# Layer B of a two-layer encoder: queries, keys and gates worked on in the projection's PSUM bank instead of in an SBUF copy

## The chip, the cores and the metric

The kernel runs on one core of one Trainium2 chip. The metric is the device time of one execution in microseconds (us). A core has five engines that run side by side, each through its own queue in order: PE (TensorE, matmuls and transposes), DVE (VectorE), ACT (ScalarE), POOL (GpSimd) and SP (SyncE, which here issues the DMAs). They wait for one another by semaphores. Matmul results land in PSUM, which PE, ACT and DVE reach and POOL does not.

## The reference

One inference step of a two-layer streaming encoder, model width 1024, on 2048 prompt frames and 64 sample frames. Layer A is gated sliding-window attention (16 query heads, 2 key heads, own chunk of 64 frames and 2 previous ones); layer B is gated chunk-band attention (16 heads of 64, own chunk and 8 previous ones, a learned bias by clipped distance). Both layers do

```
h = rms_norm(x, g);  q, k, v, gate = split(h @ w_in)
q = rms_norm(q, q_g) per head;  k = rms_norm(k, k_g) per head
o = softmax(q k^T / 8 + bias) v          (band of chunks; layer A with sinks)
y = x + (o * silu(gate)) @ w_out
```

and the newest keys and values are returned as caches. What matters here is layer B's path from the projection `h @ w_in` of 128 frames to normed queries and keys, and to silu(gate) = gate/2 * (tanh(gate/2) + 1).

## The kernel before, in words

Layer B works on 8 head pairs, one after the other. For each head pair it projects 16 prompt tiles of 128 frames (two tiles are a unit) and one sample tile of 64 frames, which comes between prompt tiles 13 and 14. A projection (`project`) is 24 matmuls of 128x512 for a prompt tile (lines 713 to 715, three products of high and low fp16 parts) and 16 for a sample tile (708, 709). Its 512 result columns are 128 of queries, 128 of keys, 128 of values and 128 of gate, for two heads. They fill one PSUM bank called `pj`, of which there are two: the projection after the next one writes the same bank again.

The result is evacuated by `evacuate_b`, for each of the 128 prompt tiles of the 8 head pairs: ACT copies queries and keys times a scale C_B into the SBUF tile `pa` (line 749, 256 columns, for the last four tiles of a head pair 384 with the values), then the high part of the values into `values` (753), then the gate times C_B into `pb` (761). DVE takes the low part of the values from PSUM (756). Behind that stands the norm, `head_norm` with `apart=True`, in three steps: POOL squares `pa` into `sq` (795); DVE sums the squares by head (809) and POOL adds a constant and raises to the power -1/2 (812, 813); DVE multiplies `pa` by the result in place (818). And the gate, in two steps: ACT takes tanh of half of `pb` into `sq` (832); DVE forms (tanh + 1) * gate in `pb` (838).

The order of the work is written out by hand on PE, where attention of one head pair and the projections of the next (the `filler`) are interleaved to marks. The other engines get their work in the order in which the code emits it. The small steps above are deferred: `bg.put` queues a step, and `bg.share`, called twice for each of the four score blocks of a unit, counts a turn up and runs due steps up to a budget of cost. A step put with `after=` comes at least one turn behind the one that it names, and `wait=2` means two turns. `bg.run` forces a step at once. The queries and keys are transposed by PE (904 called from `queries`, line 1422 on) once all steps of their unit are emitted.

Further lines that the text below uses: 1498 and 1499 are the score matmuls into the double PSUM buffer `sb`; 1502 is DVE's bias and minimum over a block of scores and 1507 its correction; 1514 is ACT's exponential; 1554 and 1555 split the weights of attention into high (ACT) and low (POOL); 500 and 503 split weights of the next projection (ACT, DVE); 1877 is a DVE operation of the output projection that reads PSUM; 1301 is the copy of the transposed gate; 222 a small matmul that spreads scales over the partitions. Layer A uses `head_norm` and `gate` too, and so does the sample tile.

Of the kernel before, what the change touches and what calls it, by code (L numbers as in the profile page):

```python
# [13 lines left out]
AF = mybir.ActivationFunctionType  # L14
ALU = mybir.AluOpType
AX = mybir.AxisListType

P = 128
# [7 lines left out]
NT = SEQ // P  # L26
NO = 8
OT = TOK // NO
HD = 64
# [20 lines left out]
HB, WB_, PB, VB = 2.0 ** 10, 2.0 ** 14, 2.0 ** 14, 16.0  # L50
LAG = 4
SQB = 4
# [4 lines left out]
def hybrid_encoder_kernel(  # L57
# [97 lines left out]

    most = const([P, 84], "most")
    top = const([P, 12], "top")
    scl = const([P, 9, 3], "scl")
    gsb = const([P, 8, KC], "gsb")
    S_W, C_B, G_B = (lambda h, i=i: scl[:, h, i : i + 1] for i in range(3))  # L160
# [26 lines left out]
    def times(dst, a, c):  # L187
        nc.vector.tensor_scalar(dst, a, c, 1.0, op0=ALU.mult, op1=ALU.mult)
# [30 lines left out]

    def everywhere(h, o):  # L220
        ps = tp_bank()
        nc.tensor.matmul(ps[:, 0:3], ones[0:1, 0:1].to_broadcast([1, P]), o, start=True, stop=True)

        def fn():
            nc.vector.tensor_copy(scl[:, h], ps[:, 0:3])
# [9 lines left out]

    def input_across(h):
        across(h, h + 1)
        e, r, o = row[:, 16:17], row[:, 17:18], row[:, 20:23]
        powers(row[:, h : h + 1], e, r)
        times(o[:, 0:1], r, WB_)  # L240
        times(o[:, 1:2], e, 1 / (HB * WB_))
        times(o[:, 2:3], e, 0.5 / VB if h > 0 and len(TURNED) == 2 else 0.5 / (VB * PB))

    def input_scales(h):
        everywhere(h, row[:, 20:23])

    def output_top():
        largest(8, 64, 80)
# [451 lines left out]

    def project(tile_, xc, w, C, res, ps=None):
        tt, t0, n = tile_
        ps = ps or psum("pj", 512, 2)
        for k in range(KC):
            wh, wl = weights_of(w, k)
            xh, xl = xc.parts[k // 2]
            if xl is None:
                nc.tensor.matmul(ps[:, :C], xh[:, k % 2, :], wh, start=k == 0, stop=False)
                nc.tensor.matmul(ps[:, :C], xh[:, k % 2, :], wl, start=False, stop=k == KC - 1)
                cost = 2 * C / 2400  # L710
            else:
                xh, xl = (a[:, k % 2, t0 : t0 + n] for a in (xh, xl))
                nc.tensor.matmul(ps[:n, :C], xh, wh, start=k == 0, stop=False)  # L713
                nc.tensor.matmul(ps[:n, :C], xh, wl, start=False, stop=False)  # L714
                nc.tensor.matmul(ps[:n, :C], xl, wh, start=False, stop=k == KC - 1)  # L715
# [29 lines left out]

    def evacuate_b(hp, tt, ps, g):
        a = t("pa", [P, 384], 4)
        true = a if tt >= NT - 4 else a[:, 0:256]
        nc.scalar.activation(true, ps[:, : true.shape[1]], AF.Identity, scale=C_B(hp))  # L749
        c = VB / (HB * WB_)  # L750
        v = ps[:, 256:384].rearrange("p (h d) -> p h d", d=HD)
        vh = held["VH"][:, tt]
        nc.scalar.activation(vh[:, :, 0:HD], v, AF.Identity, scale=c)

        def low():
            nc.vector.scalar_tensor_tensor(
                vh[:, :, HD:P], v, c, vh[:, :, 0:HD], op0=ALU.mult, op1=ALU.subtract
            )

        held["rest"].append(bg.put(0.2, low, True, wait=2))  # L760
        held["evac"] = nc.scalar.activation(g, ps[:, 384:512], AF.Identity, scale=C_B(hp)).ins
        return a

    def evacuate_sample(hp, ps, g):
        a = t("pa", [P, 384], 4)
# [565 lines left out]
    def layer_b():  # L1331
# [4 lines left out]
        def add_unit(hp, unit):  # L1336
# [23 lines left out]
            def gen():  # L1360
# [9 lines left out]
                for e, (tt, t0, n) in enumerate(tiles):  # L1370
# [3 lines left out]
                    if last:  # L1374
# [8 lines left out]
                        it.ready = True  # L1383
                        yield c
                        continue
                    pr = evacuate_b(hp, tt, out[0], it.gate[:, e])
                    it.prs.append(pr)
                    v, kn = pr[:n, 256:384], pr[:n, 128:256]
                    norm = head_norm(n, pr[:n, 0:256], apart=True)
                    it.todo += norm + gate(n, it.gate[:n, e], True)  # L1390
                    if it is its[0] and e == 0:
                        block_scales(TOK - OT)
                    if tt >= NT - 4:
                        o = (tt - (NT - 4)) * P
                        it.todo.append(
                            store_kv(1, slice(0, P), kn, v, kb_p[o : o + P, cols], vb_p[o : o + P, cols], norm[-1])
                        )
                    it.ready = e == len(tiles) - 1
                    scale_work(hp, u, e)
# [628 lines left out]
```

## Time and profile before

| what | value |
|---|---|
| time, median of 3 runs | 2118.7 us (2116.3 to 2124.02) |
| the profiled execution's own time | 2123.14 us |
| its span, first to last instruction | 2121.3 us |
| PE busy | 2046.8 us, 96% of the span |
| DVE, ACT, POOL busy | 1498.7, 1440.8, 1143.7 us |
| mean granted TensorE clock | 0.991 |

Layer B's attention, with the projections of its later head pairs beside it, takes about the stretch from 865 us to 1919 us of the span; the first 135 us of it belong to the first head pair, in which the activations are scaled and split as well. Busy times count one engine's instructions; matmuls are pipelined, so that PE can be busy without being at its peak. A line such as `PE tp L904 <- DVE pa L818: 4.5, 6, 2.4` in the view of waits means that PE's instructions of line 904 that write `tp` sat idle 4.5 us in total, 6 times, at most 2.4 us, until DVE's instruction of line 818 on `pa` ended.

### The profile page before, as it was taken

How to read it: one execution, taken by the hardware profiler on the slowest of the kernel's cores; microseconds unless marked ns; L12 is line 12 of the kernel's file. 1: busy time of each engine (PE TensorE's matmuls, PEld its weight loads, DVE VectorE, ACT ScalarE, POOL GpSimd, SP SyncE). 2: the span in 40 equal slices, each digit the busy share in tenths (PEclk: the TensorE clock that was granted, in tenths of full speed). 3: DMA queues.
4: the chain of work that ended last, by engine and by line, in shares of the span. 5: the costliest groups of instructions: out<-in, count | busy, mean ns of one | idle time of the engine just before them, and what ended most of it. 6: DMA issues, size and time to landing. Idle time of an engine off the chain costs nothing.

```text
span 2121.3 us, 40864 instructions
## 1 busy us (share of the span) xinstructions
PE 2046.8 (96%) x12951; PEld 1470.7 (69%) x12951; DVE 1498.7 (71%) x4049; ACT 1440.8 (68%) x3640; POOL 1143.7 (54%) x1621
## 2 busy tenths in 40 slices
PE   8999999999999999998999999999999999999999
PEld 6788788878888999655655555555555555557788
DVE  7778778768667554687768777787877778678542
ACT  6878878767777332466677677786867777677330
POOL 5655544433445445775367576676766767575000
PEclk9999999999999999999999999999999999999999
DMA  8856545766544666744469789897897969678763
GB/s 276 274 172 213 173 157 189 215 174 212 165 149 132 212 205 200 247 148 155 138 166 225 175 191 232 169 239 180 199 216 169 254 159 212 152 152 197 215 200 115
DMA packets 509593, 404.21 MB, mean 191 GB/s; under 512 B 302064, under 2 KB 446848, under 8 KB 509344
## 3 DMA queue, kind: packets, MB, share of 16 engines
q1 hardware_dynamic: 509376, 401.60, 70.1%
q8 instruction: 102, 1.67, 0.3%
q14 instruction: 115, 0.94, 0.1%
HBM read 257.59 MB, written 73.43 MB: 156 GB/s over the span
## 4 chain that ended last, share of the span: by engine, by line
PE 59%; DVE 12%; ACT 10%; DMA 6%; issue 6%; POOL 5%; SPq 0%; ACTq 0%; POOLq 0%; DVEq 0%
PE pj L713 10%; PE pj L715 10%; PE pj L714 10%; PE pj L1871 5%; PE pj L1873 5%; PE pj L1872 5%; PE o L1660 2%; PE sa L904 2%; PE tp L904 2%; DVE p L1502 2%; ACT values L1554 2%; PE sb L1498 2%; ACT p L1514 1%; PE sb L1499 1%; PE o L1256 1%
## 5 line engine op out<-in xcount | busy, mean ns | idle before, releaser
L713 PE MATMUL pj<-wh,xx 128*128 128x512 f16 (+2 forms) x1648 | 641.9, 389 | 6.0 <-ACT pb L736 2.3
L715 PE MATMUL pj<-wh,xx 128*128 128x512 f16 (+2 forms) x1648 | 624.3, 379 | 1.3 <-POOL xx L598 1.3
L714 PE MATMUL pj<-wh,xx 128*128 128x512 f16 x1024 | 389.4, 380 | 0.8 <-DVE wh L503 0.8
L1555 POOL TENSOR_TENSOR values<-p,values 128x640 f16<-128x640 f32 (+2 forms) x224 | 281.5, 1259 | 177.5 <-ACT values L1554 172.9
L1514 ACT ACTIVATE p<-p,nm 128x640 f32<-128x640 f32 (+5 forms) x264 | 199.3, 755 | 199.5 <-DVE nm L1507 150.3
L1871 PE MATMUL pj<-xx,wh 128*128 128x264 f32 (+1 forms) x1024 | 291.4, 285 | 8.4 <-DVE res L1877 3.9
L1872 PE MATMUL pj<-xx,wh 128*128 128x264 f32 (+1 forms) x1024 | 288.9, 282 | 0.0
L1502 DVE CUSTOM_DVE_ANT_0 p<-sb,BT 128x640 f32<-128x640 f32 (+5 forms) x272 | 196.6, 723 | 94.8 <-PE sb L1499 91.1
L714 PE MATMUL pj<-wl,xx 128*128 128x512 f32 (+1 forms) x624 | 234.6, 376 | 3.0 <-DVE wl L503 3.0
L598 POOL TENSOR_TENSOR xx<-xraw,xx 128x528 fp32r<-128x528 f32 (+4 forms) x144 | 185.4, 1305 | 90.8 <-ACT xx L597 84.1
L813 POOL TENSOR_TENSOR f<-f,mhalf 128x4 f32<-128x4 f32 (+2 forms) x187 | 190.4, 1019 | 11.8
L715 PEld LDWEIGHTS <-xx 128*128 128x128 f16 x1024 | 100.5, 98 | 124.5 <-issue 2.8
L1316 POOL TENSOR_TENSOR o<-gt,o 128x256 f32<-128x256 f32 (+1 forms) x132 | 103.6, 784 | 152.2 <-ACT p L1219 92.5
L818 DVE TENSOR_TENSOR pa<-pa,f 128x256 f32<-128x256 f32 (+3 forms) x221 | 145.6, 661 | 54.4 <-POOL f L813 49.9
L795 POOL TENSOR_TENSOR sq<-pa 128x256 f32<-128x256 f32 (+2 forms) x187 | 115.0, 615 | 115.1 <-ACT pa L749 80.1
L1219 ACT ACTIVATE p<-p,nm 128x257 f32<-128x257 f32 (+2 forms) x272 | 134.4, 497 | 47.4 <-DVE nm L1213 40.0
L714 PEld LDWEIGHTS <-xx 128*128 128x128 f16 x1024 | 100.5, 98 | 82.5 <-issue 4.7
L713 PEld LDWEIGHTS <-xx 128*128 128x128 f16 x1024 | 100.6, 98 | 80.7 <-ACT xx L597 1.5
L1554 ACT CAST values<-p 128x640 f16<-128x640 f32 (+2 forms) x224 | 147.3, 658 | 5.0
L1873 PE MATMUL pj<-xx,wl 128*128 128x264 f32 x512 | 145.8, 285 | 0.5 <-DVE wl L496 0.5
L1873 PE MATMUL pj<-xx,wh 128*128 128x264 f16 x512 | 142.7, 279 | 1.0 <-DVE wh L493 1.0
L1213 DVE CUSTOM_DVE_ANT_0 p<-sa,BT,nsink 128x256 f32<-128x256 f32 (+2 forms) x272 | 117.5, 468 | 35.7 <-PE sa L904 29.8
(282 smaller groups left out, 5028.9 us busy)
## 6 DMA issues: line engine op xcount, KB each, us to landing
xx<-xsb SPq DMA_DIRECT2D x112, 512.0 KB, 4.3
xx<-xsa SPq DMA_DIRECT2D x88, 512.0 KB, 4.7
xraw<-oga SPq DMA_DIRECT2D x64, 264.0 KB, 3.8
xraw<-ogb SPq DMA_DIRECT2D x64, 264.0 KB, 3.9
xsa<-xx SPq DMA_DIRECT2D x32, 512.0 KB, 4.3
wl<-in_w_in_b_dram SPq DMA_DIRECT2D x64, 256.0 KB, 5.0
wraw<-in_w_in_b_dram SPq DMA_DIRECT2D x56, 256.0 KB, 3.6
xraw<-in_x_dram SPq DMA_DIRECT2D x40, 256.0 KB, 4.2
```

The lines of the kernel that those rows point to most:

```text
L598: nc.gpsimd.tensor_tensor(lo, rv, wide(hi), op=ALU.subtract)
L713: nc.tensor.matmul(ps[:n, :C], xh, wh, start=k == 0, stop=False)
L714: nc.tensor.matmul(ps[:n, :C], xh, wl, start=False, stop=False)
L715: nc.tensor.matmul(ps[:n, :C], xl, wh, start=False, stop=k == KC - 1)
L813: nc.gpsimd.tensor_tensor(fv, fv, mhalf[:n, :H], op=ALU.pow)
L1502: mi = nc.vector.tensor_tensor_reduce(out=p[r, :nk], in0=S[r, o : o + nk], in1=b, op0=ALU.add, op1=ALU.min, scale=1.0, scalar=3e38, accum_ ...
L1514: ex = nc.scalar.activation(p[:n, :nk], p[:n, :nk], AF.Exp, scale=-1.0, bias=it.nm[:n, c : c + 1], accum_out=it.sm[:n, c : c + 1],)
L1554: hi = nc.scalar.copy(two[:, :, 0, :], pv)
L1555: lo = nc.gpsimd.tensor_tensor(two[:, :, 1, :], pv, two[:, :, 0, :], op=ALU.subtract)
L1871: nc.tensor.matmul(ps[:, :OT], wh, oh, start=k == 0, stop=False)
L1872: nc.tensor.matmul(ps[:, :OT], wh, ol, start=False, stop=False)
L1873: nc.tensor.matmul(ps[:, :OT], wl, oh, start=False, stop=k == KC - 1)
```

## The change

For 15 of the 16 prompt tiles of a head pair:

- ACT squares queries and keys straight from PSUM (`Square` of C_B times the column, 256 columns, into `sq`). The copy of queries and keys into `pa` goes, and POOL's squares with it. For the last four tiles of a head pair ACT still copies the values (128 columns).
- DVE's scaling, which multiplied `pa` in place, reads queries and keys from PSUM, multiplies by C_B and by the norm's factor, and writes `pa`.
- The gate's copy goes. ACT takes tanh from PSUM with a scale C_T (half of C_B), right in the evacuation; DVE forms (tanh + 1) * gate with the unscaled gate from PSUM. The missing factor C_B goes into G_B, the scale that the transposed gate is copied with.

The second prompt tile of every head pair (`tt == 1`) keeps the copy of queries and keys, POOL's squares and an SBUF copy of the gate; only its scale is taken later, as for the others. The sample tile and layer A keep what they had.

Since the norm's scaling and the gate's product now read the bank, `in_banks` keeps a list of them for each bank: at the start of a projection it forces those of the bank that this projection will write. The norm has two steps instead of three. In the line of scales, one more number is made for each head pair (8 small DVE operations on one row).

```diff
@@ input_across @@
-        times(o[:, 2:3], e, 0.5 / VB if h > 0 and len(TURNED) == 2 else 0.5 / (VB * PB))
+        times(o[:, 3:4], e, 0.5 / (HB * WB_))
+        nc.vector.scalar_tensor_tensor(
+            o[:, 2:3], e, 1 / VB if h > 0 and len(TURNED) == 2 else 1 / (VB * PB), o[:, 3:4],
+            op0=ALU.mult, op1=ALU.mult,
+        )
@@ project @@
-        ps = ps or psum("pj", 512, 2)
+        if ps is None:
+            in_banks(1)
+            ps = psum("pj", 512, 2)
+            held["pj"].append([])
@@ evacuate_b @@
-        true = a if tt >= NT - 4 else a[:, 0:256]
-        nc.scalar.activation(true, ps[:, : true.shape[1]], AF.Identity, scale=C_B(hp))
+        direct = tt not in (1,)
+        if direct:
+            sq = t("sq", [P, 256], SQB)
+            nc.scalar.activation(sq, ps[:, 0:256], AF.Square, scale=C_B(hp))
+        if tt >= NT - 4 or not direct:
+            o = 256 * direct
+            w = 384 if tt >= NT - 4 else 256
+            nc.scalar.activation(a[:, o:w], ps[:, o:w], AF.Identity, scale=C_B(hp))
...
-        held["evac"] = nc.scalar.activation(g, ps[:, 384:512], AF.Identity, scale=C_B(hp)).ins
-        return a
+        e = t("sq", [P, 256], SQB)[:, 0:P]
+        src = ps[:, 384:512]
+        if tt in (1,):
+            nc.scalar.copy(g, src)
+            src = g
+        nc.scalar.activation(e, src, AF.Tanh, scale=C_T(hp))
+
+        def product():
+            nc.vector.scalar_tensor_tensor(g, e, 1.0, src, op0=ALU.add, op1=ALU.mult)
+
+        last = [bg.put(0.2, product, True, wait=1 + 1)]
+        if tt not in (1,):
+            held["pj"][-1] += last
+        if not direct:
+            return a, head_norm(P, a[:, 0:256], apart=True) + last
+        return a, norm_ps(P, ps[:, 0:256], sq, a[:, 0:256], C_B(hp)) + last
+
+    def norm_ps(n, src, sq, dst, by):
+        H = src.shape[1] // HD
+        w = H * HD
+        fv = t("f", [P, 4], 4)[:n, :H]
+
+        def sums():
+            nc.vector.tensor_reduce(
+                fv, sq[:n, :w].rearrange("p (h d) -> p h d", d=HD), axis=AX.X, op=ALU.add
+            )
+            nc.gpsimd.tensor_tensor(fv, fv, small[:n, :H], op=ALU.add)
+            nc.gpsimd.tensor_tensor(fv, fv, mhalf[:n, :H], op=ALU.pow)
+
+        def scale():
+            nc.vector.scalar_tensor_tensor(
+                dst.rearrange("p (h d) -> p h d", d=HD), src.rearrange("p (h d) -> p h d", d=HD), by,
+                fv.unsqueeze(2).to_broadcast([n, H, HD]), op0=ALU.mult, op1=ALU.mult,
+            )
+
+        first = bg.put(0.1 * H, sums, True)
+        second = bg.put(0.1 * H, scale, True, after=first)
+        held["pj"][-1].append(second)
+        return [first, second]
+
+    def in_banks(n):
+        while len(held["pj"]) > n:
+            for it in held["pj"].pop(0):
+                bg.run(it)
@@ layer_b, gen @@
-                    pr = evacuate_b(hp, tt, out[0], it.gate[:, e])
+                    pr, norm = evacuate_b(hp, tt, out[0], it.gate[:, e])
...
-                    norm = head_norm(n, pr[:n, 0:256], apart=True)
-                    it.todo += norm + gate(n, it.gate[:n, e], True)
+                    it.todo += norm
```

How the instructions of three engines move is shown at one place, prompt tile 13 of the fourth head pair, evacuated at 1383.48 us of the profile before.

On ACT, the evacuation before; `pj` is the bank, `pa` the copy of queries, keys and values, `pb` the gate, `p` a block of scores:

```order
L749 ACTIVATE pa_18273<-pj_18184,scl 128x384
L753 ACTIVATE values_11645<-pj_18184 128x2x64
L761 ACTIVATE pb_18083<-pj_18184,scl 128x128
L1514 ACTIVATE p_18253,sm_18160<-p_18253,nm_18161 128x640
L1554 CAST values_11645<-p_18253 128x5x128
L832 ACTIVATE sq_18287<-pb_18083 128x128
L500 ACTIVATE wh_18318<-wl_18294,gsb 128x512
```

The same place after; 759 is the square, 763 the copy of the values, 780 the tanh, and 1571, 1611 and 505 are the lines 1514, 1554 and 500 of before:

```order
L759 ACTIVATE sq_18180<-pj_18093,scl 128x256
L763 ACTIVATE pa_18179<-pj_18093,scl 128x128
L767 ACTIVATE values_11646<-pj_18093 128x2x64
L780 ACTIVATE sq_18184<-pj_18093,scl 128x128
L1571 ACTIVATE p_18159,sm_18069<-p_18159,nm_18070 128x640
L1611 CAST values_11646<-p_18159 128x5x128
L505 ACTIVATE wh_18223<-wl_18200,gsb 128x512
```

The tanh moves from behind the next exponential and cast into the evacuation, where the gate's copy was.

On DVE, from the low part of the values on, before; `f` is the norm's sum or factor, `sb` the scores, `wh` and `wl` weights of a later projection:

```order
L756 SCALAR_TENSOR_TENSOR values_11645<-pj_18184,values_11645 128x2x64
L1502 ISA p_18308,nm_18161<-sb_18307,BT 128x640
L809 TENSOR_REDUCE f_18285<-sq_18284 128x4
L838 SCALAR_TENSOR_TENSOR pb_18083<-sq_18287,pb_18083 128x128
L1507 TENSOR_SCALAR nm_18161<-nm_18161 128x1
L503 SCALAR_TENSOR_TENSOR wh_18318<-wl_18294,gsb,wh_18318 128x512
L1502 ISA p_18366,nm_18364<-sb_18365,BT 128x640
L1315 TENSOR_TENSOR o_3598_18354<-o_18224,o_3598_18354 64x256 x2
L818 TENSOR_TENSOR pa_18273<-pa_18273,f_18285 128x256
```

After; 798 is the sum of squares, 770 the low part, 783 the gate's product, 805 the scaling, and 1559, 1564, 508 and 1373 are the lines 1502, 1507, 503 and 1315 of before:

```order
L798 TENSOR_REDUCE f_18186<-sq_18180 128x4
L770 SCALAR_TENSOR_TENSOR values_11646<-pj_18093,values_11646 128x2x64
L1559 ISA p_18214,nm_18070<-sb_18213,BT 128x640
L783 SCALAR_TENSOR_TENSOR pb_17993<-sq_18184,pj_18093 128x128
L1564 TENSOR_SCALAR nm_18070<-nm_18070 128x1
L508 SCALAR_TENSOR_TENSOR wh_18223<-wl_18200,gsb,wh_18223 128x512
L805 SCALAR_TENSOR_TENSOR pa_18179<-pj_18093,scl,f_18186 128x256
L1559 ISA p_18271,nm_18269<-sb_18270,BT 128x640
L1373 TENSOR_TENSOR o_3599_18259<-o_18130,o_3599_18259 64x256 x2
```

The sum moves ahead of a block of scores, and the scaling ahead of a block of scores and of two additions.

On POOL at the same place, before:

```order
L795 TENSOR_TENSOR sq_18284<-pa_18273 128x256
L1555 TENSOR_TENSOR values_11645<-p_18253,values_11645 128x5x128
L812 TENSOR_TENSOR f_18285<-f_18285,small 128x4
L813 TENSOR_TENSOR f_18285<-f_18285,mhalf 128x4
L1555 TENSOR_TENSOR values_11645<-p_18308,values_11645 128x5x128
```

After; 801 and 802 are the constant and the power, 1612 is 1555 of before, and 911 the product for the cache's keys:

```order
L801 TENSOR_TENSOR f_18186<-f_18186,small 128x4
L802 TENSOR_TENSOR f_18186<-f_18186,mhalf 128x4
L1612 TENSOR_TENSOR values_11646<-p_18159,values_11646 128x5x128
L911 TENSOR_TENSOR ko_18235<-pa_18179,kgr 128x128
L1612 TENSOR_TENSOR values_11646<-p_18214,values_11646 128x5x128
```

The squares are gone, and the power comes ahead of a split of attention weights instead of behind it. On PE the order is the same as before throughout.

More of the change, by code (lines that the diff above doesn't have):

```diff
@@ L221, in everywhere @@
         ps = tp_bank()
-        nc.tensor.matmul(ps[:, 0:3], ones[0:1, 0:1].to_broadcast([1, P]), o, start=True, stop=True)
+        w = o.shape[1]
+        nc.tensor.matmul(ps[:, 0:w], ones[0:1, 0:1].to_broadcast([1, P]), o, start=True, stop=True)
         def fn():
-            nc.vector.tensor_copy(scl[:, h], ps[:, 0:3])
+            nc.vector.tensor_copy(scl[:, h, 0:w], ps[:, 0:w])
             if h < 8:
@@ L237, in input_across @@
         across(h, h + 1)
-        e, r, o = row[:, 16:17], row[:, 17:18], row[:, 20:23]
+        e, r, o = row[:, 16:17], row[:, 17:18], row[:, 20:24]
         powers(row[:, h : h + 1], e, r)
```

9 lines of the change are left out of this document (5 added, 4 removed).

## The prediction

> **What bounds the kernel now.** I read the page first, then the busy times by stretch, then PE's waits in the two stretches of layer B.
>
> ```profile
> span 2121.3 us, 40864 instructions
> PE 2046.8 (96%) x12951; PEld 1470.7 (69%) x12951; DVE 1498.7 (71%) x4049; ACT 1440.8 (68%) x3640; POOL 1143.7 (54%) x1621
> ```
>
> PE is busy 96% of the span. The next view gives busy time by stretch (columns: length, PE, PEld, DVE, ACT, POOL, granted clock, DMA share, GB/s), first for layer B's first head pair, then for the other seven.
>
> ```profile
> 865.00:1000.00 135.00, 119.50 (x688) 69.13 (x687) 101.77 (x215) 79.28 (x197) 90.72 (x107) 0.96 0.54 178
> 1000.00:1919.00 919.00, 898.18 (x5401) 518.58 (x5399) 693.59 (x1914) 695.73 (x1747) 603.24 (x825) 1.00 0.81 191
> ```
>
> PE is idle 135.0 - 119.5 = 15.5 us in the first and 919.0 - 898.2 = 20.8 us in the second, 36 us in all. The change leaves PE's matmuls and their order as they are, so these 36 us are the most that it can bring, 1.7% of the time. On the other side there is no such ceiling: a wait that it adds in front of a projection stops PE, on which everything is queued.
>
> Whom does PE wait for? From the first stretch, then the second (us in total, times, longest):
>
> ```profile
> PE tp L904 <- ACT gt L1301: 2.7, 3, 1.2
> PE tp L904 <- DVE pa L818: 2.0, 4, 0.5
> PE sb L904 <- DVE nm L1502: 1.7, 1, 1.7
> PE pj L715 <- POOL xx L598: 1.3, 1, 1.3
> PE pj L713 <- ACT xx L597: 1.0, 1, 1.0
> ...
> PE sb L1498 <- ACT wh L500: 3.9, 3, 1.3
> PE sb L1498 <- DVE nm L1502: 3.6, 4, 1.5
> PE pj L713 <- DVE values L756: 2.1, 3, 1.0
> PE tp L222 <- DVE KB L1457: 1.9, 1, 1.9
> PE sb L1499 <- DVE q L1453: 1.6, 2, 0.9
> PE sb L1498 <- ACT values L1554: 1.1, 1, 1.1
> PE sb L1498 <- DVE f L809: 1.0, 1, 1.0
> ```
>
> Only one of them, 2.0 us, is for an operation that the change shortens: the norm's scaling (818), for which the transposes of queries and keys wait. The others are for DVE, ACT and POOL operations that stand behind shortened ones in their queues.
>
> **The change part by part.** The groups of layer B's stretch (865 to 1919 us; count, then busy us and mean ns) give the durations; 1877, on the page of all groups, is the nearest row for a wide DVE operation that reads PSUM.
>
> ```profile
> L818 DVE TENSOR_TENSOR pa<-pa,f 128x256 f32<-128x256 f32 (+1 forms) x134 | 94.5, 709 | 45.3 <-POOL f L813 45.0
> L838 DVE SCALAR_TENSOR_TENSOR pb<-sq,pb 128x128 f32<-128x128 f32 (+1 forms) x134 | 65.8, 495 | 6.3 <-ACT sq L832 5.7
> L756 DVE SCALAR_TENSOR_TENSOR values<-pj,values 128x128 f16<-128x128 f32 x127 | 36.1, 284 | 6.9 <-ACT pb L761 6.0
> L1877 DVE SCALAR_TENSOR_TENSOR res<-pj,scl,res 128x264 f32<-128x264 f32 x64 | 31.3, 490 | 70.0 <-PE pj L1873 62.3 <-DMA res<-x 7.2
> L795 POOL TENSOR_TENSOR sq<-pa 128x256 f32<-128x256 f32 (+1 forms) x135 | 83.2, 616 | 80.8 <-ACT pa L749 80.1 <-DVE pa L778 0.4 <-DMA ogb<-o 0.2
> L749 ACT ACTIVATE pa<-pj,scl 128x256 f32<-128x256 f32 (+1 forms) x127 | 63.1, 497 | 30.2 <-PE pj L715 28.5
> L761 ACT ACTIVATE pb<-pj,scl 128x128 f32<-128x128 f32 x127 | 47.1, 371 | 0.0
> L832 ACT ACTIVATE sq<-pb 128x128 f32<-128x128 f32 (+1 forms) x135 | 40.3, 304 | 1.2 <-DVE pb L778 0.7
> L813 POOL TENSOR_TENSOR f<-f,mhalf 128x4 f32<-128x4 f32 (+1 forms) x134 | 136.0, 1016 | 7.7
> L1555 POOL TENSOR_TENSOR values<-p,values 128x640 f16<-128x640 f32 (+2 forms) x215 | 268.9, 1253 | 162.4 <-ACT values L1554 159.1 <-DMA pt<-values 1.1 <-POOL ko L853 0.6
> ```
>
> *POOL* loses 120 squares of 616 ns: 74 us less. *ACT*: the square takes the place of the copy of 256 columns, at its price (749); the tanh from PSUM takes the place of the gate's copy, at its price (761, also 128 columns from PSUM with a scale tile); the old tanh (832) goes, 120 x 0.304 = 36 us; 32 copies of values stand alone now and cost some 0.27 us each more (371 ns, against about 0.1 us as the last third of a 384-column copy), 9 us. Net 27 us less. *DVE*: the product of 128 columns from PSUM at the price of 756 instead of 838: 120 x (0.495 - 0.284) = 25 us less. The scaling of 256 columns from PSUM lies between 756 (128 columns) and 1877 (264 columns); I take 0.48 us, nearer to the latter: 120 x (0.709 - 0.48) = 27 us less. The eight row operations cost about 0.1 us each, 1 us, some of it ahead of line 222's matmul.
>
> The two DVE gains rest on means. Their spread (min/median/max ns of the same stretch) is:
>
> ```profile
> L818 DVE TENSOR_TENSOR pa<-pa,f x134: 280/425/1625, 879.7 to 1912.1; 128x256 f32<-128x256 f32 x126, 128x128 f32<-128x128 f32 x8
> L838 DVE SCALAR_TENSOR_TENSOR pb<-sq,pb x134: 215/292/1507, 877.6 to 1912.0; 128x128 f32<-128x128 f32 x126, 128x64 f32<-128x64 f32 x8
> ```
>
> Half of them run at 425 and 292 ns; the mean comes from some that last over a microsecond, as with a hindrance from outside. If the hindrance stays, the product gains nothing (292 against 284) and the scaling loses 120 x (0.48 - 0.425) = 7 us. So DVE's part lies between 7 us more and 52 us less. I take the latter, for the PSUM-reading operations show no such tail: 756 and 1877 have 284 and 490 ns as means for 128 and 264 columns.
>
> The Trainium skill (VectorE: DVE Perf Modes, Rules for kernel authors, and the errata table) speaks against this part: elementwise work on a matmul's output should be copied to SBUF first where several operations follow, and an operation from PSUM has a fixed cost of 120 cycles against 58 from SBUF, at 0.96 GHz 65 ns more. By that page alone, an estimate, 240 operations would cost DVE 16 us more, PE's waits for DVE would not shrink, and the time would be 2119 us.
>
> All this is beside PE's path. What of it reaches PE? The wait for 818 goes, 2.0 us: the norm has two turns instead of three, so the scaling is ready a turn earlier. The wait for 756 (2.1 us) stays, for its forced step, at the head of a head pair, is unchanged. The ten other waits quoted sum to 19.8 us. Their engines get lighter by 52 of 795 us (DVE), 27 of 775 (ACT) and 74 of 694 (POOL). A queue that is rarely late gains more than its share of work, so I take a third, 6.6 us, with nothing and all 19.8 us as the ends. Together 8.6 us off.
>
> *The new wait.* The scaling and the product must now be done before the projection after next starts in the same bank. Queued behind PE's first matmul there is all of PE's work. Prompt tile 13 of the fourth head pair is a tight place, for a short sample projection stands between; the timeline has
>
> ```profile
> 1383.48 0.58 ACT L749 ACTIVATE pa<-pj,scl 128x384 f32<-128x384 f32 x1 [0.15 <-PE pj L715]
> 1385.59 0.29 DVE L756 SCALAR_TENSOR_TENSOR values<-pj,values 128x128 f16<-128x128 f32 x1
> 1387.66 0.74 DVE L503 SCALAR_TENSOR_TENSOR wh<-wl,gsb,wh 128x512 f16<-128x512 f32 x1
> 1390.10 0.43 DVE L818 TENSOR_TENSOR pa<-pa,f 128x256 f32<-128x256 f32 x1
> 1387.81 1.46 POOL L813 TENSOR_TENSOR f<-f,mhalf 128x4 f32<-128x4 f32 x1
> 1389.14 0.38 PE L713 MATMUL pj<-wh,xx 128*128 128x512 f16 x1
> ```
>
> Before, the scaling ended at 1390.5, 1.4 us after the bank's next projection had started (1389.14): kept at that place in the queue it would have cost PE that much. In the new order it stands right behind 503, which ended at 1388.4; with 0.48 us it ends at 1388.9, 0.2 us in time. Its factor: the sum now stands ahead of 756, ends at about 1386.0, and POOL adds and raises by 1387.8, even at 1.46 us for the power. The next tile, last but one of the head pair, is the other tight place:
>
> ```profile
> 1404.41 1.14 DVE L503 SCALAR_TENSOR_TENSOR wh<-wl,gsb,wh 128x512 f16<-128x512 f32 x1
> 1405.48 0.28 DVE L838 SCALAR_TENSOR_TENSOR pb<-sq,pb 128x128 f32<-128x128 f32 x1
> 1407.10 0.41 DVE L818 TENSOR_TENSOR pa<-pa,f 128x256 f32<-128x256 f32 x1
> 1405.99 0.38 PE L713 MATMUL pj<-wh,xx 128*128 128x512 f16 x1
> ```
>
> There product, 503 and scaling end at about 1406.1 to 1406.3, 0.1 to 0.3 us late. I did this sum for the tiles of all head pairs (DVE's place in the new order, POOL's queue, the projection's start of before). As an estimate, about ten tiles are late, by 3 us together; some two dozen have under 0.45 us to spare (the two places above and two or three more in each head pair); the middle one has 2.3 us. I take 3 us, with 0 and 9 us as ends (an extra 0.25 us at each tight tile).
>
> The sum: 8.6 - 3 = 5.6 us off the profiled execution's 2123.1 us, which is 0.2% over the median of 2118.7; set against the median, 2113 us. The unknowns allow from +9 - 2 = 7 us more to 22 us less. A measurement of this kernel tells a difference of about 0.5%, 10.6 us, from none.
>
> **The rivals.**
>
> *The bank is held too long.* If the factor comes later than in my sum by one 1555 on POOL (1.25 us), because that split is taken up just before the sum ends, or the scaling by one long DVE operation, then PE stops 1.1 us at each of 24 tight tiles and 0.3 us at nine more: 29 us, less the 8.6 gained, 2139 us. It decides from 19 us of new waits on, 0.8 us at each tight tile. For it: before, the scaling missed that moment at the two places shown, by 1.1 and 1.5 us, and DVE idled 45.0 us for POOL's factor (the row of 818). Against it: the turn saved, and the power now ahead of the split. The Trainium skill (PSUM — Partial Sum Buffer, Summary: rules for kernel authors) asks to evacuate promptly, and its page Perfetto Trace Analysis (Identifying Performance Opportunities) reads repeated equal gaps as too few buffers; that would be this case. Chance 0.11.
>
> *The relief reaches PE in full.* All 19.8 us and the 2.0 us go, with no new wait: 22 us off, 2097 us. For it: three engines together lose 150 us, and POOL's squares no longer stand ahead of the splits. Against it: PE's idle time in the second stretch is 2% already, scattered over many causes, several of them weights and transfers. From half of it on this counts as faster. Chance 0.24.
>
> *Nothing reaches PE.* The change takes work off engines that PE hardly waits for, the means of 818 and 838 turn into equal hindrance elsewhere, and gains and new waits cancel: 2119 us. Chance 0.13.
>
> **How the numbers follow.** My forecast, 2108 to 2118, has 0.52. Faster by over 0.5% (under 2108.1) is the full relief, 0.24, with the forecast's edge, 0.02: 0.26. Slower by over 0.5% (over 2129.3) is the held bank: 0.11. Within 0.5%: 0.63. The range goes from 2101 to 2126 us: the lower end takes in most of the full relief's side, the upper end the 7 us more of the unknowns; outside are some 0.09 below and 0.11 above.
>
> **What would show it.** In the profile after: 805 at about 0.48 us and 783 at 0.28 us without long ones; no POOL squares but those of the sample, of the second tiles and of layer A; the transposes' wait for the scaling gone; PE's waits of 713 and 708 for the DVE lines 805 and 783 at 0 to 9 us in all; PE idle by some 5 us less, most of it in the first head pair's stretch. Wrong would be the forecast if PE's waits for line 805 reached 1 us at the tight tiles, repeated in each head pair, or if PE's idle time fell by half.

## The result, and the profile after

After takes 2100.26 us (median of 4 runs, 2099.73 to 2104.95), before beside it 2120.55 us (2116.3 to 2124.02). The ratio is 0.991, 95% interval 0.9886 to 0.9935: 0.9% faster, well beyond the 0.5% that can be told from no change. On the 2118.7 us of the prediction this is 2099.6 us (2094.5 to 2104.9). The forecast of 2113 us was too timid: the measured value lies 1.4 us below its range of 2101 to 2126 us, into which only the upper part of its interval reaches.

The page of after, span and busy times (the profiled execution took 2099.98 us):

```profile
span 2098.2 us, 40785 instructions
PE 2034.6 (97%) x12951; PEld 1465.1 (70%) x12951; DVE 1444.2 (69%) x4057; ACT 1420.6 (68%) x3552; POOL 1070.0 (51%) x1501
```

DVE has 54.5 us less, ACT 20.2, POOL 73.7 (forecast 52, 27 and 74). PE issues the same 12951 matmuls in the same order, and yet is busy for 12.2 us less. To see where, the span is cut at the same matmuls in both kernels. First before, then after: layer A, layer B's first head pair, its other seven, the stretch behind them (the last head pair's end and the output projection), and the end. Columns as in the prediction.

```profile
0.00:865.00 865.00, 838.32 (x5206) 719.99 (x5207) 601.53 (x1731) 593.59 (x1567) 424.37 (x662) 0.99 0.63 195
865.00:1000.00 135.00, 119.50 (x688) 69.13 (x687) 101.77 (x215) 79.28 (x197) 90.72 (x107) 0.96 0.54 178
1000.00:1919.00 919.00, 898.18 (x5401) 518.58 (x5399) 693.59 (x1914) 695.73 (x1747) 603.24 (x825) 1.00 0.81 191
1919.00:2000.00 81.00, 73.29 (x620) 60.97 (x619) 55.81 (x114) 49.38 (x97) 25.42 (x29) 0.96 0.77 201
2000.00:2121.30 121.30, 117.54 (x1045) 101.99 (x1043) 46.03 (x81) 22.84 (x35) 0.00 (x0) 1.00 0.55 166
```

```profile
0.00:861.30 861.30, 835.32 (x5206) 716.99 (x5207) 600.73 (x1732) 592.89 (x1567) 424.83 (x662) 0.99 0.64 195
861.30:993.20 131.90, 117.38 (x688) 68.39 (x687) 91.81 (x216) 75.66 (x186) 79.19 (x95) 0.97 0.56 178
993.20:1902.30 909.10, 894.44 (x5400) 518.04 (x5399) 652.53 (x1922) 681.69 (x1674) 542.20 (x720) 1.00 0.83 193
1902.30:1976.90 74.60, 69.96 (x620) 59.70 (x619) 53.15 (x111) 47.56 (x94) 23.75 (x26) 1.00 0.84 218
1976.90:2098.20 121.30, 117.50 (x1045) 101.95 (x1042) 45.95 (x81) 22.80 (x35) 0.00 (x0) 1.00 0.56 167
```

Length minus PE's busy time is PE's idle time. It fell by 0.7 us in layer A, 1.0 in the first head pair, 6.2 in the other seven and 3.1 in the stretch behind: 10.9 us with rounding. PE's busy time fell by 3.0, 2.1, 3.7 and 3.3 us in the same stretches: 12.2 us. So of the 23.1 us between these two executions 10.9 us are idle time. Most of the rest is clock: the clock falls to a half in windows of 3.41 us, each of which takes away 1.7 us; before has 11 of them in its trace (5, 3, 1 and 2 in the first four stretches), after 5 (3, 2, 0 and 0), and six are 10.2 us. The last 2.0 us of PE's busy time, in the seven later head pairs, are not explained.

The groups that the prediction priced, in after's layer B:

```profile
L805 DVE SCALAR_TENSOR_TENSOR pa<-pj,scl,f 128x256 f32<-128x256 f32 x119 | 57.3, 482 | 39.5 <-POOL f L802 37.5
L783 DVE SCALAR_TENSOR_TENSOR pb<-sq,pj 128x128 f32<-128x128 f32 x119 | 33.0, 278 | 0.0
L759 ACT ACTIVATE sq<-pj,scl 128x256 f32<-128x256 f32 x119 | 55.9, 470 | 22.6 <-PE pj L723 21.7
L780 ACT ACTIVATE sq<-pj,scl 128x128 f32<-128x128 f32 x119 | 44.3, 372 | 0.0
```

And the spread of the scaling (min/median/max ns):

```profile
L805 DVE SCALAR_TENSOR_TENSOR pa<-pj,scl,f x119: 470/484/486, 875.0 to 1900.5; 128x256 f32<-128x256 f32 x119
```

PE's waits in the seven later head pairs of after, to be held against the second group of waits in the prediction:

```profile
PE sb L1555 <- DVE nm L1559: 7.1, 6, 1.5
PE pj L721 <- DVE nm L1564: 2.1, 4, 0.5
PE sb L1555 <- DMA q<-q: 0.9, 1, 0.9
PE pj L721 <- DVE values L770: 0.8, 2, 0.5
PE pj L721 <- DVE pa L805: 0.6, 1, 0.6
```

The waits for 500 (3.9 us), 1457 (1.9), 1453 (1.6), 1554 (1.1) and 809 (1.0) are gone from the head of this view, and that for 756 (now 770) fell from 2.1 to 0.8. New are those of `pj` for the bank, five places, 2.7 us of idle time together (805; or 1564, the DVE instruction right behind it, which the view names where it ended last). The wait of the scores for DVE (1502, now 1559) grew from 3.6 to 7.1. The new wait looks like this in the timeline of after, at tile 14 of the fourth head pair (the second place of the prediction):

```profile
1391.41 0.28 DVE L783 SCALAR_TENSOR_TENSOR pb<-sq,pj 128x128 f32<-128x128 f32 x1
1391.61 1.92 DVE L508 SCALAR_TENSOR_TENSOR wh<-wl,gsb,wh 128x512 f16<-128x512 f32 x1
...
1393.45 0.47 DVE L805 SCALAR_TENSOR_TENSOR pa<-pj,scl,f 128x256 f32<-128x256 f32 x1
...
1394.07 0.38 PE L721 MATMUL pj<-wh,xx 128*128 128x512 f16 x1 [0.53 <-DVE nm L1564]
```

Product, weight remainder (508, the old 503) and scaling stand in the order that the prediction read; the remainder took 1.92 us, and the projection starts behind the scaling. Its first matmul starts 0.91 us behind the one before it, where matmuls of this shape otherwise start every 0.22 us: 0.69 us are lost, of which the view counts 0.53 as idle. The same 0.69 us stands at this tile in five head pairs, 3.5 us in all.

### The profile page after: what moved, and what is told of

It reads as the page before. It is cut to its first block, busy times and chain, and to the rows that moved or that the text cites. A ratio compares the mean times of both kernels' runs of the same rounds, so it can differ in the third digit from the quotient of the medians.

```text
span 2098.2 us, 40785 instructions
## 1 busy us (share of the span) xinstructions
PE 2034.6 (97%) x12951; PEld 1465.1 (70%) x12951; DVE 1444.2 (69%) x4057; ACT 1420.6 (68%) x3552; POOL 1070.0 (51%) x1501
## 4 chain that ended last, share of the span: by engine, by line
PE 67%; DVE 10%; ACT 7%; issue 6%; DMA 6%; POOL 3%; SPq 1%; ACTq 0%; POOLq 0%; DVEq 0%
PE pj L721 12%; PE pj L723 12%; PE pj L722 12%; PE pj L1928 4%; PE pj L1930 4%; PE pj L1929 4%; PE o L1717 3%; PE tp L962 2%; PE sa L962 2%; PE sb L1555 2%; PE sb L1556 2%; POOL xx L603 1%; DVE p L1559 1%; DVE wh L508 1%; PE o L1314 1%
## 5 line engine op out<-in xcount | busy, mean ns | idle before, releaser
L1271 DVE CUSTOM_DVE_ANT_0 p<-sa,BT,nsink 128x256 f32<-128x256 f32 (+2 forms) x272 | 117.5, 468 | 33.7 <-PE sa L962 28.3
L723 PEld LDWEIGHTS pj<-wh,xx 128*128 128x128 f32 x624 | 118.0, 189 | 22.9
L721 PEld LDWEIGHTS pj<-wh,xx 128*128 128x128 f32 x624 | 118.3, 190 | 22.0 <-ACT pb L744 4.1
L722 PEld LDWEIGHTS pj<-wl,xx 128*128 128x128 f32 x624 | 118.8, 190 | 18.1 <-DVE wl L508 3.4
```

## The experiments

Three theories at first. *Relief*: DVE, POOL and ACT reach the work that PE waits for sooner. *The turn*: the norm in two steps instead of three is the gain. *The parts*: norm and gate each bring their own. All ratios below are to before, from runs on the same chip. The kernels came on several chips, so they are compared by their ratios.

| kernel | us | ratio, 95% interval |
|---|---|---|
| after | 2100.26 | 0.9910 (0.9886 to 0.9935) |
| early_norm | 2138.25 | 1.0087 (1.0069 to 1.0105) |
| norm_only | 2107.48 | 0.9938 (0.9919 to 0.9958) |
| gate_only | 2113.03 | 0.9975 (0.9961 to 0.9989) |
| load_back | 2119.69 | 1.0004 (0.9992 to 1.0015) |
| pool_back | 2114.84 | 0.9987 (0.9967 to 1.0006) |
| dve_back | 2109.41 | 0.9956 (0.9940 to 0.9972) |
| act_back | 2099.41 | 0.9909 (0.9882 to 0.9936) |
| pool_load | 2107.03 | 0.9947 (0.9928 to 0.9966) |
| pool_pow | 2115.90 | 0.9987 (0.9969 to 1.0005) |
| two_exceptions | 2102.38 | 0.9929 (0.9903 to 0.9955) |
| no_exception | 2130.08 | 1.0055 (1.0035 to 1.0075) |
| late_norm | 2106.30 | 0.9936 (0.9912 to 0.9959) |

**The turn alone** (before, with POOL's squares emitted at once):

```diff
         first = bg.put(0.15 * H - 0.1 * apart, squares, True)
...
+        if early:
+            bg.run(first)
         second = bg.put(0.1 * H, sums, True, after=first)
```

> The kernel before with one thing moved: for layer B's prompt tiles POOL's squares are emitted at once in the evacuation, so that the norm takes two turns instead of three. All copies, squares, the gate and all loads stay as before. Theory of the turn (what was gained is that the transposes of queries and keys no longer wait for the norm): 2101 to 2107 us, 0.992 to 0.995 of before, and PE's wait of tp for the scaling under 0.5 us. Theory of the relief (what was gained is lighter queues on DVE, ACT and POOL): 2117 to 2122 us, no difference from before, other PE waits as before.

It is 0.9% slower. Groups of its layer B, and two of PE's waits there:

```profile
L795 POOL TENSOR_TENSOR sq<-pa 128x256 f32<-128x256 f32 (+1 forms) x133 | 81.7, 614 | 107.9 <-ACT pa L749 105.7 <-DVE pa L778 1.7
L818 DVE TENSOR_TENSOR pa<-pa,f 128x256 f32<-128x256 f32 (+1 forms) x132 | 117.2, 888 | 56.6 <-POOL f L813 54.6 <-DMA xx<-xsb 0.9
```

```profile
PE sb L1500 <- DVE nm L1504: 14.0, 9, 2.4
...
PE tp L906 <- DVE pa L818: 2.1, 3, 1.5
```

POOL now stands still 105.7 us for ACT's copy (before 80.1), with the splits queued behind it, and the scaling from SBUF got longer, 888 ns against 709. PE pays for it at the scores: its wait for DVE's bias and minimum (1504, before 1502) went from 3.6 to 14.0 us. The wait of the transposes for the scaling, which the turn should have ended, is still 2.1 us. So as an edit of before the turn is no gain. What it would bring without POOL's longer stop this kernel can't show; late_norm, below, comes nearer to that.

**The parts.** norm_only keeps before's gate, gate_only before's norm (`direct = False` for all tiles).

> The change's norm alone: squares and scaling from PSUM, in two turns; the gate is copied to SBUF, its tanh and product deferred as before. Theory of the turn: all of the gain, 2099 to 2105 us, with the new wait for the bank as in the full change. Theory of the relief: POOL is lighter by 74 us and DVE by 27 of its 54, ACT not; some half of the gain, 2108 to 2113 us.

> The change's gate alone: tanh in the evacuation and product, both from PSUM; queries and keys are copied to SBUF and normed there in three turns as before. Theory of the turn: no gain, 2117 to 2122 us, since the scaling is as late as before. Theory of the relief: DVE lighter by 25 us and ACT by 36, some half of the gain, 2108 to 2113 us.

0.62% and 0.25% add up to 0.87%, about as much as after's 0.90%. The norm part takes off all of POOL's 74 us and more than half of DVE's (DVE 1468.9 us busy, of after's 1444.2 and before's 1498.7), the gate part 21 us of DVE's and 22 us of ACT's. The traces put the gain on the norm's side: cut at the same matmuls, the seven later head pairs take 910.3 us in norm_only, close to after's 909.1, but 920.2 us in gate_only, no less than before's 919.0. Where gate_only's 0.25% comes from its one trace does not show.

**All load given back** (after, with a POOL product, a DVE product and an ACT copy for each direct tile):

```diff
+        def again():
+            nc.gpsimd.tensor_tensor(spare, sq, sq, op=ALU.mult)
+            nc.vector.tensor_tensor(spare2, sq, sq, op=ALU.mult)
+            nc.scalar.copy(spare3, sq[:, 0:P])
+        third = bg.put(0.0, again, True, after=first)
+        held["pj"][-1].append(third)
```

> The changed kernel with the relief given back: in the turn after the sums, for each of the 120 tiles, POOL squares 256 columns, DVE multiplies 256 columns (both inputs in SBUF) and ACT copies 128 columns, into spare tiles that nobody reads. Order and turns of all else stay. Theory of the turn: as the changed kernel, 2098 to 2104 us. Theory of the relief: most of the gain is lost, 2112 to 2121 us.

Nothing of the gain is left. But the view of waits shows it lost in another place than it was won (1565 and 1569 are after's 1555 and 1559, 1574 its 1564):

```profile
PE pj L721 <- DVE pa L805: 9.1, 9, 1.3
PE sb L1565 <- DVE nm L1569: 8.0, 6, 1.7
PE pj L721 <- DVE nm L1574: 4.6, 5, 0.9
```

PE waits 13.7 us for the bank, after 2.7. In the seven later head pairs PE is idle 28.3 us, more than before's 20.8: the loads cost more there than the change had won. Since the loads stood in the list that must be emitted ahead of the bank's next projection, this part of the loss may come from the experiment itself. The next kernels put the load behind the scaling, in no list, one engine at a time.

**One engine's load.** In `scale()`, behind the scaling; one line for each kernel, with its name behind it:

```diff
+            nc.gpsimd.tensor_tensor(spare, spare, spare, op=ALU.mult)                # pool_back
+            nc.vector.tensor_tensor(spare[:, 0:192], spare[:, 0:192], spare[:, 0:192], op=ALU.mult)  # dve_back
+            nc.scalar.copy(spare3[:, 0:32], spare[:, 0:32])                          # act_back
+            nc.gpsimd.tensor_tensor(spare, sq, sq, op=ALU.mult)                      # pool_load
+            nc.gpsimd.tensor_tensor(spare[:, 0:4], sq[:, 0:4], mhalf[:, 0:4], op=ALU.pow)  # pool_pow
```

> After, with a product of 256 columns on POOL behind each scaling of layer B's prompt tiles (118 times, its result unused, nothing waits for it): POOL alone gets back some 75 of the 74 us it had lost, DVE and ACT keep their relief. Three theories of where after's 20 us came from. 'DVE's relief': PE's waits that went had mostly named DVE lines, so POOL's load costs little: 2101 to 2104 us. 'POOL's relief': the squares no longer stand ahead of the factor and the splits, so most comes back: 2110 to 2116 us. 'All by their load' (74, 54 and 20 us of 148): half of the 20 us comes back, 2110 us. 'Held bank' (the kernel with all three loads back was slow because its loads stood ahead of the bank's release): with no release behind the load none of the three moves by more than 3 us.

> After, with a product of 192 columns on DVE behind each scaling of layer B's prompt tiles (118 times, result unused): DVE alone gets back some 55 us. 'DVE's relief': most comes back, 2110 to 2118 us, with PE's waits naming DVE lines up by 8 us or more. 'POOL's relief': 2101 to 2105. 'All by their load': 7 us of the 20, 2107 us. 'Held bank': under 3 us.

> After, with a copy of 32 columns on ACT behind each scaling of layer B's prompt tiles (118 times, some 0.2 us each, result unused): ACT alone gets back some 25 us, a little more than the 20 it had lost. 'DVE's relief' and 'POOL's relief': 2100 to 2103. 'All by their load': 3 us of the 20, 2103. 'Held bank': under 3 us. Rival 'ACT's relief' (the waits for the attention's probabilities and the splits of weights are ACT's): 2108 to 2114.

pool_back says nothing on layer B. Its product depends on no tile, and was run in layer A: POOL's time up to 865 us, in after (first row) and pool_back (second), rose by 72 us there.

```profile
0.00:865.00 865.00, 839.02 (x5226) 718.91 (x5227) 602.83 (x1737) 594.07 (x1569) 426.34 (x664) 0.99 0.64 196
0.00:865.00 865.00, 831.28 (x5148) 711.34 (x5149) 614.94 (x1722) 589.99 (x1562) 498.25 (x776) 0.99 0.62 192
```

All 120 products ran between 2.9 and 237 us of its span. The kernel is 0.8% slower than after all the same, but not in layer B: its seven later head pairs take 909.1 us, as in after, and layer A 872.3 us instead of 861.3.

The loads of dve_back and act_back depend on no tile either, but all but two or three of their 120 instructions ran from 865 us on. ACT's load costs nothing that these runs can tell: its relief has no part in the gain that they show. DVE's load (63.3 us by the profile; DVE's whole busy time rose by 44.6 us) gives back about 9 of the 19 us, a part of it at the bank (these two waits together 6.6 us, after 2.7):

```profile
PE pj L721 <- DVE nm L1567: 4.3, 5, 0.9
...
PE pj L721 <- DVE pa L805: 2.3, 4, 0.8
```

> After, with a product of 256 columns of the squares on POOL behind each scaling of layer B's prompt tiles (result unused; it reads the tile's squares, so unlike the product in pool_back it can't be started before layer B): POOL gets back some 73 us in layer B. dve_back gave back 9 of after's 19 us, act_back none. 'POOL's queue': the product stands ahead of the splits and of the next factor, most of the other 10 us come back, 2108 to 2112 us. 'POOL and DVE at SBUF together': the same size, 2108 to 2112, with DVE's own SBUF operations (the weights' remainders, 508) longer than after's 1.02 us mean. 'POOL has no part': 2099 to 2103 us; then what load_back gave back beyond dve_back is the bank's release that stood behind its loads.

> The same kernel with a power of 128x4 in the place of the product of 256 columns: it holds POOL for longer (about 1.0 us each, 123 us in all) but moves 64 times fewer elements. 'POOL's queue': worse than pool_load, 2112 to 2120 us. 'POOL and DVE at SBUF together': next to nothing comes back, 2100 to 2104 us. 'POOL has no part': 2099 to 2103 us.

Both keep the load in layer B, and the order is that of POOL's queue: the product (73.5 us) gives back 0.37%, its interval just overlapping after's, and the power, longer but with 64 times fewer elements, 0.77%. The weights' remainders did not lengthen, 1028 and 1029 ns, and DVE is busy for the same 652.5 us in the seven later head pairs of after, pool_load and pool_pow, to within 0.2 us. So the theory of contention at SBUF falls. The group of the load and PE's wait for the bank, first in pool_load:

```profile
L809 POOL TENSOR_TENSOR spare<-sq 128x256 f32<-128x256 f32 x119 | 73.5, 618 | 77.0 <-ACT sq L759 72.7 <-DMA xsb<-xx 3.3
```

```profile
PE pj L721 <- DVE pa L805: 4.7, 4, 1.4
```

Then in pool_pow:

```profile
L809 POOL TENSOR_TENSOR spare<-sq,mhalf 128x4 f32<-128x4 f32 x119 | 120.5, 1012 | 76.1 <-ACT sq L759 75.2
```

```profile
PE pj L721 <- DVE pa L805: 10.9, 8, 1.6
```

One of the eight places in pool_pow's timeline:

```profile
1403.30 0.19 POOL L801 TENSOR_TENSOR f<-f,small 128x4 f32<-128x4 f32 x1
1403.44 1.39 POOL L1614 TENSOR_TENSOR values<-p,values 128x640 f16<-128x640 f32 x1
...
1404.80 1.00 POOL L802 TENSOR_TENSOR f<-f,mhalf 128x4 f32<-128x4 f32 x1
...
1405.83 0.48 DVE L805 SCALAR_TENSOR_TENSOR pa<-pj,scl,f 128x256 f32<-128x256 f32 x1 [1.19 <-POOL f L802]
...
1406.46 0.38 PE L721 MATMUL pj<-wh,xx 128*128 128x512 f16 x1 [1.50 <-DVE pa L805]
```

A split (1614, before 1555) stands between the addition and the power, the factor comes 1.4 us later, and PE stops 1.5 us for the bank. That is the mechanism of the first rival. In after, at the same tile, the power follows the addition and the split comes behind it, and PE does not stop. So the load also changes the order on POOL: something stands between addition and power for 12 of the 120 factors of after, for 27 in pool_load and for 29 in pool_pow. POOL's relief is therefore, for a good part, what pays for the bank being held.

DVE's 9 us and the 8 us of pool_load, each for about the load that the change had taken off, together come near the 19. About 4 us of each are waits for the bank, though, which before did not have; so this shows that the gain hangs on light DVE and POOL queues, and not that the same waits were won. The theory of the relief is the one that fits best, for DVE and POOL; how the gain divides between the two is not shown.

**The bank's deadline.** no_exception makes the second tile of each head pair direct too (`tt not in ()`); two_exceptions takes tile 14 back to SBUF as well (`tt not in (1, 14)`); late_norm puts the scaling one turn later (`wait=2`).

> After, with the second tile of each head pair direct too, which the change leaves on the way through SBUF. 'Held bank': before, the scaling of that tile ended some 7 us after the bank's next projection had started, in most head pairs; moved ahead of it, DVE's queue there costs PE 1 to 3 us in each of 7 or 8 head pairs: 8 to 20 us slower than after, 2108 to 2120 us, with PE's wait for line 805 at that place. 'Relief alone': one more tile in 15 direct, 1 us faster, 2099 us.

> After, with the last but one tile of each head pair (tile 14) also by way of SBUF, so that its bank comes free as early as before. 'Held bank' (the wait of 0.69 us at tile 14 of five head pairs, 3.5 us in all, is a loss of its own): 3 to 5 us faster than after, 2096 us, PE's wait for the DVE lines of scaling and product at 'pj' gone. 'Relief': 8 tiles more of the old work (about 0.23 us of DVE's, 0.6 of POOL's and 0.2 of ACT's time each) give back a fifteenth of the 20 us, 1.3 us, at a place that is tight already, and the wait moves on to the next tile: 2099 to 2102 us.

> After, with the scaling put one turn later. 'Held bank': the scaling comes as late as before, which missed the bank's next projection by 1.1 and 1.5 us at the two places of the prediction; 0.8 to 1 us at each of some 24 tight tiles, 2115 to 2125 us. 'Forced order': the queue runs the scaling at the latest before the projection that needs its bank, so that at tight tiles little changes: 2100 to 2106 us. 'The turn': the earlier scaling is itself the gain, through the transposes of queries and keys: 2103 to 2108 us, with PE's waits of 962 for 805 back at 2 us or more.

no_exception is 1.5% slower than after, for a single tile in 16. Its wait, its timeline at one of the six places, and busy times around that place:

```profile
PE pj L721 <- DVE pa L805: 19.7, 6, 3.5
```

```profile
1296.93 0.48 DVE L805 SCALAR_TENSOR_TENSOR pa<-pj,scl,f 128x256 f32<-128x256 f32 x1 [0.62 <-POOL f L802]
...
1297.47 0.39 PE L721 MATMUL pj<-wh,xx 128*128 128x512 f16 x1 [3.25 <-DVE pa L805]
```

```profile
1295.40:1298.80 3.40, 1.33 (x7) 0.66 (x8) 1.40 (x6) 1.65 (x3) 3.02 (x5) 1.00 1.01 374
1298.80:1302.20 3.40, 3.40 (x18) 2.46 (x17) 1.15 (x3) 0.48 (x1) 0.76 (x1) 0.50 0.07 24
```

PE stops 3.25 us, and then runs 3.4 us at half the clock: each stop costs 3.3 us and at least 1.7 more. The trace has eight such windows at the six stops, which take away 13.7 us beside the 19.7 us of waiting; after has none in these head pairs. That is the held bank at its full price, more than the 8 to 20 us expected, because the clock was not in the sum. The exception that the change makes for this tile is worth about 30 us.

two_exceptions and after can't be told apart (0.9929 and 0.9910, intervals overlapping). In its trace the 0.69 us of tile 14 are gone at five places, and come back at others:

```profile
PE pj L721 <- DVE values L770: 2.6, 6, 1.0
...
PE pj L721 <- DVE pa L805: 1.7, 3, 0.7
```

late_norm lies between: 0.26% above after, with overlapping intervals. The 'held bank' expectation of 2115 to 2125 us falls, because the code forces the scaling ahead of the projection that needs the bank; the waits for the bank (805 and 1564) grew from 2.7 to 5.4 us only. The sign of 'the turn' did not come either: the transposes (962) wait 0.2 us for 805, where 2 us or more were expected, although the scaling again comes two turns behind the norm's first step, as in before. The seven later head pairs take 911.3 us, 2.2 more than in after. So if the turn has a part of its own in the gain, it is small; by the times it lies between nothing and 0.6%.

## Why the prediction was right or wrong

*What bounds the kernel* was right in direction and wrong as a bound. "These 36 us are the most that it can bring" took PE's busy time as given. It is not: with the same matmuls it fell by 12.2 us, 10.2 of them because fewer matmuls ran at half the clock. Here is the longest such place of before, between 1986 and 1996 us, and the same work in after:

```profile
1986.00:1989.40 3.40, 1.29 (x12) 0.98 (x10) 1.11 (x2) 1.47 (x2) 0.00 (x0) 1.00 0.94 297
1989.40:1992.80 3.40, 2.52 (x12) 1.72 (x12) 1.22 (x3) 0.00 (x0) 0.00 (x0) 0.50 0.72 233
1992.80:1996.20 3.40, 3.40 (x18) 2.23 (x16) 0.45 (x1) 0.00 (x0) 0.00 (x0) 0.50 0.39 105
```

```profile
1965.70:1969.10 3.40, 2.47 (x22) 2.00 (x21) 1.83 (x3) 2.21 (x3) 0.00 (x0) 1.00 1.03 297
1969.10:1972.50 3.40, 2.46 (x22) 2.15 (x22) 1.28 (x3) 0.00 (x0) 0.00 (x0) 1.00 0.99 289
```

Before, PE stopped there for 3.0 us, after for 1.9 us, and the two half-clock windows did not come. Part of the difference between these two executions is chance (layer A, which the change hardly touches, has 3.0 us of it, and takes between 857 and 865 us in the traces of all kernels but pool_back). But not all: the mean granted clock of the 74 runs of before made beside the experiments is 0.9928, that of after's four 0.9958, and 0.3% of 2119 us is some 6 us. The runs of before say the same: those 13 with a clock of 0.995 to 0.997, as after has it, took 2113 us on average, so that 13 us of the difference remain at equal clock. So about 6 of the 19 us are clock, a term that the sum did not have. What raised the clock is not isolated: load_back has 0.9955 on average, as much as after, and none of the gain.

*The operations' prices* held. Scaling 482 ns (taken 480) and product 278 (284), without a tail: 470 to 486 ns where the scaling from SBUF went from 280 to 1625. DVE lost 54.5 us (52), POOL 73.7 (74), ACT 20.2 (27).

The Trainium skill (VectorE: DVE Perf Modes, Rules for kernel authors) leaves a choice for elementwise work on a matmul's output, to read it from PSUM at the lower rate or to copy it to SBUF first where many operations follow. The prediction's estimate from that page, 16 us more for DVE and 2119 us, took the second half alone, and does not come out here: the scaling's mean from PSUM is lower by 227 ns, since it has no long ones. The fixed cost in the page's errata table, 65 ns more from PSUM by the prediction's estimate, fits the scaling's median (484 against 425 ns), not the product's (277 against 292).

*The other waits.* "A third" of 19.8 us, 6.6, with the 2.0 of the transposes, less 3 us, made 5.6 us less idle time. In layer B it fell by 7.1 us (1.0 + 6.2, rounded), close to that. The nearness is in part luck, for the net hides two larger terms: the scores' wait for DVE (1502) grew by 3.5 us, which the sum had falling, and five others in the second group of waits, 9.5 us, left the head of the view. But its place was wrong: "most of it in the first head pair's stretch", while 6.2 of it came from the seven others. And the sum ended at 1919 us; the stretch behind it, left out, gave 3.1 us of idle time more. They come again in the other traces: cut at the same matmuls, this stretch has 7.1 to 7.7 us of idle time in before, early_norm, gate_only and load_back, and 4.2 to 5.7 in after, act_back, pool_back, norm_only, late_norm and two_exceptions.

*The turn.* "The wait for 818 goes": the transposes' wait for the scaling, 2.0 us in the first head pair, is gone in after. But the reason given, a turn saved, is not borne out: in early_norm, with the turn saved, the wait is still 2.1 us, and in late_norm, with the turn given back, it is 0.2 us.

*The new wait* was right: 3.5 us measured, 3 taken, and at the second place shown, where 0.1 to 0.3 us was expected and 0.69 came, because 508 took 1.92 us. The first place, forecast 0.2 us in time, shows no stop in after. (The rival's text has the scaling of before 1.1 us late there; by the lines shown it is 1.4 us, as the paragraph on the new wait says.)

*The rivals.* The full relief gave the right time, 2097 us, by a mechanism that was at most half right, and so in part by luck: of its 22 us of waits 7 went, net; the clock gave about 6 and the stretch behind 3. The held bank did not come, but it is real: 8 stops of up to 1.6 us with 120 us more on POOL, and 30 us for one tile too many. Its price per place (1.1 us) was too low where the clock falls as well.

So the step that failed is the first one, which took layer B's idle time for all that could be won. The ceiling of 36 us itself was not reached; the terms that were mis-sized are the clock, some 6 us instead of 0, and the stretch behind 1919 us, 3 us instead of 0. Why the clock rose stays open.

## What to carry to other kernels

Where PE is busy 96% of the time, look at the clock column too: idle time that is spread over short stops also costs clock, so adding a stop can cost more than its length (no_exception), and taking one away can bring more. Working in a PSUM bank takes copies off three engines but sets them a deadline; the engines whose queues produce and apply the last factor, here POOL and DVE, decide if it is met, and one tile at the wrong place can undo the whole. A test load should depend on data of the stage in which it is meant to run, or it may run elsewhere, as pool_back's did, and its trace has to show whether it left the order of the other work alone.

## What the hardware showed that was not expected

The half clock comes in windows on a fixed grid. In the trace of before they begin at 30.2, 84.8, 217.9, 439.8, 767.5, 873.3, 958.6, 1811.9 and 1989.4 us, all multiples of 3.4133 us apart to within 0.02 us (84.8 - 30.2 is 16 of them, 217.9 - 84.8 is 39), and last one or two such windows. What goes with it is how busy PE was in the window before. At 1811.9 us there was no long stop:

```profile
1808.50:1811.90 3.40, 1.54 (x9) 0.50 (x7) 2.71 (x6) 2.62 (x10) 1.23 (x2) 1.00 1.01 264
1811.90:1815.30 3.40, 3.40 (x15) 2.07 (x14) 0.87 (x5) 1.78 (x4) 0.00 (x0) 0.51 0.04 11
```

PE's longest stop in that window was 1.0 us; several of them left it busy for 1.54 us. In the traces of before, after and no_exception, from 15 us on, each drop from the full clock followed a window with 0.2 to 1.7 us of PE work, and windows with more than that kept it (in after two with 1.4 and 1.6 us kept it too). The edge is not sharp by this measure: load_back has a drop behind a window with 2.25 us, so that busy time alone does not decide. The Trainium skill (TensorE: Matmul & The Clock Gate, What's actually happening) states a free-running window of 3413 ns, whose length these traces confirm; its advice in "Why this matters for your kernels" to avoid idle gaps over some 3 us is too lenient here, since gaps of at most 1.0 us were enough. On such a grid, whether a given stop costs 1.7 us more depends on where it falls. That fits the spread between the 74 runs of before, 2107.31 to 2129.08 us: their time follows their mean clock (correlation -0.83), from 2124 us on average for the 12 runs at 0.989 or 0.990 to 2113 us for the 13 at 0.995 to 0.997. That the place of the stops on the grid makes this difference was not tested.
